# Tying gate units to attention steps, with three smaller moves around them, in a hybrid decoder trunk

## Chip, cores and metric

One Trainium2 chip, one of its cores. The metric is the device time of one launch in microseconds (us), the median of several runs. The engines are called PE (matrix multiplication), DVE (VectorE), ACT (ScalarE), POOL (GpSimd) and SP (SyncE, which here only issues transfers).

## What is computed

One layer of a decoder, for 1024 prompt tokens (NP) and 64 sample tokens (NS) that share the weights. All matrices are float32; the kernel multiplies them as sums of float16 parts, so each matrix product of weights is three matmuls per 128 rows.

```
h = x + 0.5 * g1 * SwiGLU_1(rms(x) * (1 + sc1) + sh1)
u = rms(h) * (1 + sc2) + sh2
[q | k | v | s | ga | gb] = u @ w_in
a = stick-breaking attention(q, k, v)         8 heads x 64, strictly causal
b = GLU(gelu(S5 diagonal SSM(s)))
h = h + g2 * ((sigmoid(ga) * (a @ w_branch_a) + sigmoid(gb) * (b @ w_branch_b)) @ w_out)
h = h + 0.5 * g3 * SwiGLU_2(rms(h) * (1 + sc3) + sh3)
y = final_rms(h)
```

## The kernel before

The program runs as one chain of stages: the first SwiGLU (to about 770 us), the mixer with its projections, SSM, gated linear unit and attention (`mixer_a`, to 1506 us), the mixer's branch products and w_out (`mixer_b`), the second SwiGLU. The order of instructions on each engine is made by a scheduler from the program's order and its dependencies; `tc.issue_after(x)` makes it place what is traced inside behind instruction x. Every engine then runs its own list strictly in that order.

**Weights.** The class `Weights` (L106) holds a list of weight groups. `fetch` loads one by SP into `wf` (two buffers), `measure` takes its largest value (DVE L89, POOL L82, then three small DVE instructions L74 to L76 that make a power-of-two scale), and a split writes `wh` (ACT L101) and `wl` (DVE L102), again two buffers each. `ahead()` brings the next groups to that state.

**Gate units.** The gates ga and gb are 16 units of 128 columns, two to a weight group. `project` (inside `mixer_a`) traces one unit: three chunks of tokens, each 24 matmuls `u<-u,wh` or `u<-u,wl` (L226), 72 in all; ACT evicts each chunk with `gate<-u` (L1339), and a transfer stores it to `gd` in memory (L1340). The 16 units fill holes of other stages: some stand beside the SSM, two before and one inside the gated linear unit (`between`), the remaining eleven go to the attention loop.

**SSM.** `ssm_run` runs in four blocks. Each ends with eight transfers `m<-gp` (L976) that fetch a matrix, matmuls `z<-u,m` (L988, L990), ACT evictions `y<-z` (L992), and eight transfers `yd<-y` (L995) that store the block's result. Both sets of transfers are issued by SP.

**Gated linear unit.** `glu` reads the SSM's result, applies gelu (`zg`), takes its largest value (`zm`), makes the scale `sz` (L74 to L76), splits `zg` into `z` (ACT and DVE L101, L102), and multiplies by two weight groups `glu_w` (PE L226).

**Attention.** `attend_prompt` runs four pairs of heads, two blocks of 512 queries each, and 4 or 8 blocks of keys in each: 48 steps. A step is: logits `z<-qs,kT` (PE L1087, with the causal mask L1092), two evictions by ACT `ae<-z` (L1094) and one each by ACT (L1096) and DVE (L1098), exp and log (ACT L1012, L1013), two DVE instructions (L1014, L1015), a float16 split (ACT L1017, DVE L1021), sums over keys `P<-ah,tri` (PE L1024), `az<-P` (DVE L1026), exp (ACT L1028), sums carried to the next step `P<-ah,earlier` (PE L1103), and the output `o<-az,vt` (PE L1108). Steps overlap: the logits of the next step can run while the last two are still on ACT and DVE. `attend_sample` is traced in pieces between steps.

**The loop around it** pops a gate unit whenever fewer units were popped than the share of steps done times a constant; what is left when the attention ends is traced after it:

```
    while n_gates - len(gates) < (n_gates - 3) * done / steps:
        gates.pop(0)()
```

**Branch products.** `mixer_b` multiplies first branch b (`ob`), then branch a, in units of 36 matmuls (`unit`, L216), with two units in PSUM. Each unit's gate is loaded (`sg<-gd`), ACT applies the sigmoid (L1491), and DVE multiplies product and gate into `mt` (L1495), which frees the unit's PSUM.

Of the kernel before, what the change touches and what calls it, by code (L numbers as in the profile page):

```python
# [9 lines left out]
F32 = mybir.dt.float32  # L10
# [10 lines left out]
P = 128  # L21
# [19 lines left out]
GC = 16  # L41
# [28 lines left out]
def pow2_scale(k, m, pool=None, tag="sc", bufs=8, lead=14):  # L70

    nc = k.nc
    sc = (pool or k.small).tile([P, 2], F32, tag=tag, bufs=bufs)
    nc.vector.tensor_single_scalar(sc[:, 1:2].bitcast(I32), m.bitcast(I32), 0x7F800000, op=ALU.bitwise_and)  # L74
    nc.vector.tensor_scalar(sc[:, 1:2], sc[:, 1:2], 2.0 ** -100, 2.0 ** -lead, op0=ALU.max, op1=ALU.mult)
    nc.vector.reciprocal(sc[:, 0:1], sc[:, 1:2])  # L76
    return sc[:, 0:1], sc[:, 1:2]
# [187 lines left out]
def c3(t):  # L265
    return t.rearrange("p (c n) -> p c n", c=3)
# [642 lines left out]
def ssm_run(k, par, bt, st, ds):  # L909
# [82 lines left out]
            nc.scalar.activation(y.rearrange("p (a g) c -> p g a c", g=2)[:, g2, gas[0]:gas[-1] + 1, :],  # L992
                                 p[:, :len(gas), :], AF.Copy)
    for j in range(TC):
        nc.sync.dma_start(ds["y"][bt, :, j, :].rearrange("(g h) c -> h g c", h=GC), y[GC * j:GC * j + GC])  # L995
    yield


# [70 lines left out]
def attend_prompt(k, qT, kT, vt, pairs, scales):  # L1069

    nc = k.nc
    for p in pairs:
        qs, ks, inv, c = scales[p]
        for qc in range(2):
            acc = k.psa.tile([P, 2, 512], F32, tag="P")
            po = k.pso.tile([P, 512], F32, tag="o")
            top = 4 * qc + 3
            for j in range(top, -1, -1):
                q0 = max(0, P * j - 512 * qc)
                n = 512 - q0  # L1080
                cols = slice(512 * qc + q0, 512 * qc + 512)

                def logits(az, ae):
                    pz = [k.psz.tile([P, 512], F32, tag="z") for _ in range(2)]
                    for i in range(2):
                        for h, ps in enumerate(pz):
                            nc.tensor.matmul(ps[:, :n], ks[:, h, P * j:P * j + P], qs[:, h, i, cols], start=i == 0,  # L1087
                                             stop=True, skip_group_check=True)
                    for h, ps in enumerate(pz):
                        b = k.bias[:, 2 * p + h:2 * p + h + 1]  # L1090
                        if j >= 4 * qc:
                            nc.tensor.matmul(ps[:, :P], k.ident16, k.causal, start=False, stop=True,  # L1092
                                             skip_group_check=True)
                        nc.scalar.activation(ae[:, h, :n], ps[:, :n], AF.Abs, scale=inv, bias=b)  # L1094
                        if h:
                            nc.scalar.activation(az[:, h, :n], ps[:, :n], AF.Identity, scale=inv, bias=b)  # L1096
                        else:
                            nc.vector.tensor_scalar(az[:, h, :n], ps[:, :n], inv, b, op0=ALU.mult, op1=ALU.add)  # L1098

                def rest(hi, lo):  # L1100
                    for h in range(2):
                        for part in (hi, lo):
                            nc.tensor.matmul(acc[:, h, q0:], k.earlier, part[:, h, :], start=False, stop=True,  # L1103
                                             skip_group_check=True)

                w = weights_of(k, n, 2, P, acc[:, :, q0:], logits, rest if j else None, None, j == top, c)
                for h in range(2):
                    nc.tensor.matmul(po[64 * h:64 * h + 64, q0:], vt[:, j, (2 * p + h) * DH:(2 * p + h + 1) * DH],  # L1108
                                     w[:, h, :], start=j == top, stop=j == 0, skip_group_check=True)
                if (qc, j) == (1, 3) and p < 3:  # L1110
                    scales.append(scaled_pair(k, qT, kT, p + 1, (k.qkv, k.ring)[(p + 1) % 2]))
                if j:
                    yield
            o = qT[:, p, 512 * qc:512 * qc + 512]
            nc.scalar.activation(o, po, AF.Copy)
            absmax(k, o, k.mo[:, 2 * p + qc:2 * p + qc + 1])
            yield
# [160 lines left out]
def mixer_a(k, dr, out, u, ivu, par, ds, gd, od):  # L1278
# [6 lines left out]
    def project(g, q, sink, last=False):  # L1285
        if q == 0:
            cur["w"] = k.w.next()
            cur["iv"] = mul_small(k, cur["w"][1], ivu)
        f = sink(2 * g + q, cur["iv"])
        unit_chunks(k, cur["w"], slice(q * P, q * P + P), act, KD, f)  # L1290
        if q and not last:
            k.w.ahead()
# [47 lines left out]
            (nc.gpsimd if m == 15 else nc.sync).dma_start(gd[m, :, c * CH:(c + 1) * CH], t)  # L1340
        return f

    gates = [lambda g=g, q=q: project(g, q, to_gate, g == 7) for g in range(8) for q in range(2)]
    k.gate_slot = lambda: k.ring.tile([P, CH], F32, tag="gs", bufs=2, name="gate")

    def between():
        gates.pop(0)()

    run(2, keep(kT))
    nc.sync.dma_start(out["kT"].rearrange("m p t -> p m t"), kT)  # L1350
# [23 lines left out]
    k.cs_qk = k.co.tile([P, 4, 3], F32, tag="csqk")  # L1374
    k.part_slot = lambda: k.ring.tile([P, NP], F16, tag="r", name="hs")
    scales = [scaled_pair(k, qT, kT, 0, k.qkv)]
    for _ in range(2):
        between()
    ivb = glu(k, dr, ds, od, between)
    k.part_slot = lambda: k.ring.tile([P, 2, 512], F16, tag="h", bufs=4, name="hs").rearrange("p a b -> p (a b)")  # L1380
    first.close()
# [10 lines left out]
    sample = attend_sample(k, dr, qT, kT, vt)  # L1392
    for _ in attend_prompt(k, qT, kT, vt, range(4), scales):
        done += 1
        while n_gates - len(gates) < (n_gates - 3) * done / steps:
            gates.pop(0)()
        if done % 4 == 0:
            next(sample, None)
    for _ in sample:
        pass  # L1400
    for f in gates:
        f()

    n = NP + NS
    s, inv = pow2_scale(k, allmax(k, absmax(k, k.mo)), k.co, "so", 1)
# [7 lines left out]
def glu(k, dr, ds, od, between):  # L1413
# [9 lines left out]
    for m in range(4):  # L1423
# [7 lines left out]
        absmax(k, z, zm[:, 0, m:m + 1])  # L1431
        zg.append(z)
    s, ivz = pow2_scale(k, allmax(k, absmax(k, zm[:, 0, :])), k.co, "sz", 1)
    for m in range(4):
        z2.append(slot([P, 2, T], F16, "z2"))
        split(k, z2[m][:, 0, :], z2[m][:, 1, :], zg[m], s)
# [20 lines left out]
def mixer_b(k, oa, ivo, od, ivb, gd, x, xd, gate, after_chunk):  # L1457
# [25 lines left out]
    for branch, ivx in ((1, ivb), (0, ivo)):  # L1483
        for g in range(2):
            w = k.w.next()
            iv = mul_small(k, w[1], ivx)
            for q in range(4):
                m = 4 * g + q
                sg = k.ring.tile([P, T], F32, tag="r", name="sg")
                nc.sync.dma_start(sg, gd[8 * branch + m])  # L1490
                nc.scalar.activation(sg, sg, AF.Sigmoid)  # L1491
                ps = unit(k, w, slice(q * P, q * P + P), operand[branch], 4)
                if branch:
                    merged.append(slot([P, T], F32, "mt"))
                    v.scalar_tensor_tensor(c3(merged[m]), ps, iv, c3(sg), op0=ALU.mult, op1=ALU.mult)  # L1495
                else:
                    v.scalar_tensor_tensor(c3(sg), ps, iv, c3(sg), op0=ALU.mult, op1=ALU.mult)
                    v.tensor_add(merged[m], merged[m], sg)
                    absmax(k, merged[m], mm[:, m:m + 1])
            if not branch:  # L1500
                half(g)
        if branch:
            for c in range(3):
                nc.sync.dma_start(x[:, :, c * CH:(c + 1) * CH], xd[:, :, c * CH:(c + 1) * CH])
# [323 lines left out]
```

## Time and profile before

| | us |
|---|---|
| median of 3 runs | 2433.33 (2432.96 to 2435.21) |
| profiled execution, its own time | 2430.38 |
| its span | 2428.7 |
| PE busy | 2300.0 (95%) |
| DVE busy | 1663.9 (69%) |
| ACT busy | 966.2 (40%) |
| mean granted clock of PE | 0.977 of full |

Shares of busy time are means over stages. A stage is read from stretches of the span: how long each engine is busy in it, and which wait ends last there. The granted clock is 1.00 at 2.4 GHz and 0.50 at 1.2 GHz; a value between is a stretch with some of each.

### The profile page before, as it was taken

The page shows a single profiled execution, that of the slowest core. Times are in us where ns is not written, and L with a number is a line of the kernel's source. Part 1 is how long each engine was busy: PE and PEld are TensorE (multiplying, and loading weights), DVE is VectorE, ACT ScalarE, POOL GpSimd, SP SyncE. Part 2 cuts the span into 40 slices and gives each one's busy share as a digit, 9 for nine tenths or more (in the row PEclk, how much of TensorE's full clock was granted, in tenths as well). Part 3 has the DMA queues.
Part 4 walks back from the last instruction along what each step waited for, and adds up shares of the span by engine and source line. Part 5 has one row for each costly group of instructions (what it writes and reads, how often), then busy time and mean ns, then how long its engine had stood idle before and what let it go on. Part 6 is the DMA issues. An engine that isn't in the chain of part 4 may idle for free.

```text
span 2428.7 us, 42932 instructions
## 1 busy us (share of the span) xinstructions
PE 2300.0 (95%) x18439; PEld 1631.1 (67%) x18439; DVE 1663.9 (69%) x2994; ACT 966.2 (40%) x1233; POOL 142.3 (6%) x193
## 2 busy tenths in 40 slices
PE   5999999899999999997999977999999999999997
PEld 2677778677787666684545523555688878888884
DVE  4776588877787526435788877597487655677735
ACT  3533331233332422134788877333443321333403
POOL 0000000000000000000332300000000000000000
PEclk8999999999999999998999988999999999999998
DMA  8132334432342154452344413522111133211302
GB/s 306 53 122 101 114 118 140 149 118 109 134 154 105 53 176 112 131 186 102 114 119 131 147 36 110 183 87 86 43 53 53 44 124 109 79 57 53 127 18 75
DMA packets 94191, 262.83 MB, mean 108 GB/s; under 512 B 13152, under 2 KB 50400, under 8 KB 83760
## 3 DMA queue, kind: packets, MB, share of 16 engines
q1 hardware_dynamic: 88240, 242.46, 29.3%
q0 software_dynamic: 5312, 17.34, 2.4%
q8 instruction: 144, 2.36, 0.4%
q14 instruction: 47, 0.39, 0.1%
q10 hardware_dynamic: 448, 0.29, 0.0%
HBM read 204.10 MB, written 49.66 MB: 104 GB/s over the span
## 4 chain that ended last, share of the span: by engine, by line
PE 59%; DVE 11%; ACT 5%; DMA 4%; issue 3%; POOL 1%; SPq 1%; DVEq 0%; POOLq 0%; ACTq 0%
PE u L477 20%; PE u L242 14%; PE u L226 13%; PE u L216 3%; PE z L1364 2%; DVE wl L102 1%; DVE mx L89 1%; DMA wf<-in_w_in 1%; PE P L1024 1%; PE z L990 1%; PE o L1108 1%; PE z L226 1%; ACT ae L1094 1%; PE z L1151 1%; DMA aw<-in_ada_w 1%
## 5 line engine op out<-in xcount | busy, mean ns | idle before, releaser
L226 PE MATMUL u<-u,wh 128*128 128x364 f16 (+1 forms) x1632 | 388.4, 319 | 9.6 <-ACT u L394 6.3
L242 PE MATMUL u<-h,wh 128*128 128x272 f16 (+1 forms) x2304 | 366.8, 281 | 5.2 <-DVE h L102 5.2
L101 ACT ACTIVATE wh<-wf,sc 128x1024 f16<-128x1024 f32 (+2 forms) x128 | 182.4, 1427 | 377.0 <-PE u L242 168.9
L242 PEld LDWEIGHTS <-wh 128*128 128x128 f16 x2816 | 273.8, 97 | 66.1 <-issue 9.0
L89 DVE TENSOR_REDUCE mx<-wf 128x1 f32<-128x1024 f32 (+2 forms) x134 | 211.0, 1597 | 153.0 <-DMA wf<-in_ffn_w_in 78.0
L102 DVE SCALAR_TENSOR_TENSOR wl<-wf,sc,wh 128x1024 f16<-128x1024 f32 (+2 forms) x128 | 208.8, 1631 | 97.7 <-ACT wh L101 97.2
L477 PE MATMUL u<-u,wh 128*128 128x272 f16 x1728 | 273.2, 280 | 0.3 <-DVE q L499 0.3
L477 PEld LDWEIGHTS <-wh 128*128 128x128 f16 x2304 | 221.5, 97 | 64.1 <-issue 20.3
L226 PEld LDWEIGHTS <-wh 128*128 128x128 f16 x1824 | 176.9, 98 | 130.4 <-issue 28.9
L226 PE MATMUL u<-u,wl 128*128 128x364 f16 (+1 forms) x816 | 259.9, 319 | 1.1 <-DVE wl L102 1.1
L242 PE MATMUL u<-h,wl 128*128 128x274 f16 (+1 forms) x1152 | 228.8, 280 | 0.0
L477 PEld LDWEIGHTS <-w3h 128*128 128x128 f16 x1728 | 167.1, 97 | 39.0 <-issue 4.5
L477 PE MATMUL u<-fac,w3h 128*128 128x272 f16 (+1 forms) x1152 | 182.7, 280 | 0.0
L477 PE MATMUL u<-u,wl 128*128 128x272 f16 x864 | 170.5, 279 | 0.0
L82 POOL PARTITION_ALL_REDUCE am<-mx x106 | 55.7, 532 | 1924.8 <-DVE mx L89 1845.5
L242 PEld LDWEIGHTS <-wl 128*128 128x128 f16 x1408 | 136.8, 97 | 29.6
L226 PEld LDWEIGHTS <-wl 128*128 128x128 f16 x912 | 89.3, 98 | 61.0 <-issue 6.9
L477 PEld LDWEIGHTS <-wl 128*128 128x128 f16 x1152 | 111.6, 97 | 24.5 <-issue 0.4
L226 PEld LDWEIGHTS <-aside 128*128 128x128 f16 x864 | 83.0, 97 | 50.5 <-issue 1.7
L477 PE MATMUL u<-fac,w3l 128*128 128x272 f16 x576 | 114.0, 279 | 0.0
L503 ACT ACTIVATE h<-h,iv 128x546 f32<-128x546 f32 x36 | 27.0, 749 | 205.8 <-DVE h L502 205.8
L477 PE MATMUL u<-fac,wh 128*128 128x272 f16 x576 | 92.3, 283 | 4.7 <-DVE st L519 4.7
(429 smaller groups left out, 3893.1 us busy)
## 6 DMA issues: line engine op xcount, KB each, us to landing
wf<-in_ffn_w_in SPq DMA_DIRECT2D x44, 1024.0 KB, 4.7
aw<-in_ada_w SPq DMA_DIRECT2D x72, 512.0 KB, 4.6
wf<-in_w_in SPq DMA_DIRECT2D x16, 1024.0 KB, 5.0
wf<-in_ffn_w_out_a SPq DMA_DIRECT2D x16, 640.0 KB, 4.0
xd<-xr SPq DMA_DIRECT2D x16, 546.0 KB, 2.7
x<-xd SPq DMA_DIRECT2D x16, 546.0 KB, 7.3
xd<-x SPq DMA_DIRECT2D x6, 1456.0 KB, 7.4
sg<-gd SPq DMA_DIRECT2D x16, 546.0 KB, 3.6
```

Of the source, the lines that this page charges most:

```text
L82: k.nc.gpsimd.partition_all_reduce(r, m, P, ABSMAX)
L89: k.nc.vector.tensor_reduce(m, src, axis=axis, op=ALU.max, apply_absolute_value=True)
L101: r = k.nc.scalar.activation(hi, src, AF.Copy, scale=s)
L102: k.nc.vector.scalar_tensor_tensor(lo, src, s, hi, op0=ALU.mult, op1=ALU.subtract)
L216: k.nc.tensor.matmul(ps[:, c, :n], wt[:, cols], act(kt, part)[:, c * CH:c * CH + n], start=kt == 0 and j == 0, stop=kt == nk - 1 and j == 2)
L226: k.nc.tensor.matmul(ps[:, :n], wt[:, cols], act(kt, part)[:, c * CH:c * CH + n], start=kt == 0 and j == 0, stop=kt == nk - 1 and j == 2)
L242: k.nc.tensor.matmul(ps[:, a:b], wt[:, cols], act(kt, part)[:, a0 + a:a0 + b], start=kt == 0 and j == 0, stop=kt == nk - 1 and j == 2)
L477: nc.tensor.matmul(t[:, c0:c1], wt[:, kt * P:kt * P + P], act(kt, part)[:, c0 - 240:c1 - 240], start=first and kt == 0 and j == 0, stop=kt ...
L503: nc.scalar.activation(h2, h2, AF.Silu, scale=iv)
L990: nc.tensor.matmul(p[:, q, :], ca[rows, ri, ga, 1:, :].rearrange("p a b -> p (a b)"), x[rows, ga, :], start=False, stop=ri == 1)
L1024: nc.tensor.matmul(acc[:rk, h, :], k.tri[:rk, :rk], part[:, h, :], start=first and j == 0, stop=True, skip_group_check=True)
L1364: nc.tensor.matmul(ps[:M, :256], u[:, kt, part, tt * P:tt * P + M], wt, start=kt == 0 and j == 0, stop=kt == KD - 1 and j == 2)
```

## The change

Four edits. (1) The SSM's stores `yd<-y` are issued by ACT instead of SP. (2) `attend_prompt` remembers the last logits matmul it traced (`k.anchor`), and a gate unit popped in the attention loop is placed behind it; the loop's constant changes so that nine units are popped inside and two after it, and these two are tied to the last logits as well. (3) The second unit before the gated linear unit no longer requests weights; `glu` does that itself once it has made `sz`. (4) In branch b, the first two units are evicted by ACT into `mt` with the scale, and the gate is multiplied in later; a tile `gap` takes 128 columns of the ring.

```diff
--- before.py
+++ after.py
@@ -992,7 +992,7 @@
             nc.scalar.activation(y.rearrange("p (a g) c -> p g a c", g=2)[:, g2, gas[0]:gas[-1] + 1, :],
                                  p[:, :len(gas), :], AF.Copy)
     for j in range(TC):
-        nc.sync.dma_start(ds["y"][bt, :, j, :].rearrange("(g h) c -> h g c", h=GC), y[GC * j:GC * j + GC])
+        nc.scalar.dma_start(ds["y"][bt, :, j, :].rearrange("(g h) c -> h g c", h=GC), y[GC * j:GC * j + GC])
     yield
 
 
@@ -1084,8 +1084,8 @@
                     pz = [k.psz.tile([P, 512], F32, tag="z") for _ in range(2)]
                     for i in range(2):
                         for h, ps in enumerate(pz):
-                            nc.tensor.matmul(ps[:, :n], ks[:, h, P * j:P * j + P], qs[:, h, i, cols], start=i == 0,
-                                             stop=True, skip_group_check=True)
+                            k.anchor = nc.tensor.matmul(ps[:, :n], ks[:, h, P * j:P * j + P], qs[:, h, i, cols],
+                                                        start=i == 0, stop=True, skip_group_check=True).ins
                     for h, ps in enumerate(pz):
                         b = k.bias[:, 2 * p + h:2 * p + h + 1]
                         if j >= 4 * qc:
@@ -1340,11 +1340,11 @@
             (nc.gpsimd if m == 15 else nc.sync).dma_start(gd[m, :, c * CH:(c + 1) * CH], t)
         return f
 
-    gates = [lambda g=g, q=q: project(g, q, to_gate, g == 7) for g in range(8) for q in range(2)]
+    gates = [lambda g=g, q=q, last=False: project(g, q, to_gate, last or g == 7) for g in range(8) for q in range(2)]
     k.gate_slot = lambda: k.ring.tile([P, CH], F32, tag="gs", bufs=2, name="gate")
 
-    def between():
-        gates.pop(0)()
+    def between(**kw):
+        gates.pop(0)(**kw)
 
     run(2, keep(kT))
     nc.sync.dma_start(out["kT"].rearrange("m p t -> p m t"), kT)
@@ -1374,8 +1374,8 @@
     k.cs_qk = k.co.tile([P, 4, 3], F32, tag="csqk")
     k.part_slot = lambda: k.ring.tile([P, NP], F16, tag="r", name="hs")
     scales = [scaled_pair(k, qT, kT, 0, k.qkv)]
-    for _ in range(2):
-        between()
+    between()
+    between(last=True)
     ivb = glu(k, dr, ds, od, between)
     k.part_slot = lambda: k.ring.tile([P, 2, 512], F16, tag="h", bufs=4, name="hs").rearrange("p a b -> p (a b)")
     first.close()
@@ -1392,14 +1392,16 @@
     sample = attend_sample(k, dr, qT, kT, vt)
     for _ in attend_prompt(k, qT, kT, vt, range(4), scales):
         done += 1
-        while n_gates - len(gates) < (n_gates - 3) * done / steps:
-            gates.pop(0)()
+        while n_gates - len(gates) < (n_gates - 2) * done / steps:
+            with tc.issue_after(k.anchor):
+                gates.pop(0)()
         if done % 4 == 0:
             next(sample, None)
     for _ in sample:
         pass
     for f in gates:
-        f()
+        with tc.issue_after(k.anchor):
+            f()
 
     n = NP + NS
     s, inv = pow2_scale(k, allmax(k, absmax(k, k.mo)), k.co, "so", 1)
@@ -1431,6 +1433,7 @@
         absmax(k, z, zm[:, 0, m:m + 1])
         zg.append(z)
     s, ivz = pow2_scale(k, allmax(k, absmax(k, zm[:, 0, :])), k.co, "sz", 1)
+    k.w.ahead()
     for m in range(4):
         z2.append(slot([P, 2, T], F16, "z2"))
         split(k, z2[m][:, 0, :], z2[m][:, 1, :], zg[m], s)
@@ -1488,10 +1491,18 @@
                 m = 4 * g + q
                 sg = k.ring.tile([P, T], F32, tag="r", name="sg")
                 nc.sync.dma_start(sg, gd[8 * branch + m])
-                nc.scalar.activation(sg, sg, AF.Sigmoid)
                 ps = unit(k, w, slice(q * P, q * P + P), operand[branch], 4)
                 if branch:
+                    if m == 0:
+                        k.ring.tile([P, 128], F32, tag="gap", bufs=1)
                     merged.append(slot([P, T], F32, "mt"))
+                early = branch and m < 2
+                if early:
+                    nc.scalar.activation(c3(merged[m]), ps, AF.Copy, scale=iv)
+                nc.scalar.activation(sg, sg, AF.Sigmoid)
+                if early:
+                    v.tensor_mul(merged[m], merged[m], sg)
+                elif branch:
                     v.scalar_tensor_tensor(c3(merged[m]), ps, iv, c3(sg), op0=ALU.mult, op1=ALU.mult)
                 else:
                     v.scalar_tensor_tensor(c3(sg), ps, iv, c3(sg), op0=ALU.mult, op1=ALU.mult)
```

How the lists of the engines move is shown at three places.

ACT, fourth pair of heads, second block of queries, from the exp of the 384-wide step on; `ae<-z` is the eviction of a step's logits, `gate<-u` that of a gate chunk. Before:

```order
L1012 ACTIVATE ae<-ae 128x2x384
L1094 ACTIVATE ae<-z,bias,csqk 128x512
L1013 ACTIVATE ae<-ae 128x2x384
L1094 ACTIVATE ae<-z,bias,csqk 128x512
L1028 ACTIVATE az<-az 128x2x256
L1096 ACTIVATE az<-z,bias,csqk 128x512
L1017 ACTIVATE ah<-ae,csqk 128x2x384
L1012 ACTIVATE ae<-ae 128x1024
```

And now:

```order
L1012 ACTIVATE ae<-ae 128x2x384
L1013 ACTIVATE ae<-ae 128x2x384
L1339 ACTIVATE gate<-u,iv 128x364
L1028 ACTIVATE az<-az 128x2x256
L1017 ACTIVATE ah<-ae,csqk 128x2x384
L1028 ACTIVATE az<-az 128x2x384
L1339 ACTIVATE gate<-u,iv 128x364
L101 ACTIVATE wh<-wf,sc 128x2048
L1339 ACTIVATE gate<-u,iv 128x364
L1094 ACTIVATE ae<-z,bias,csqk 128x512 x2
```

The steps in flight now run to their last exp (`az<-az`), and the three chunks of a gate unit are evicted, before the next step's logits. On PE the 72 gate matmuls of such a unit stand in the same place: behind one step's logits, between the `P` and `o` matmuls of the steps in flight, and all before the logits of the next. There are eight such units; the last gate matmuls in a row directly before the next logits are 36, 2, 49, 3, 25, 18, 31 and 24. Before, gate matmuls stood spread among logits, `P` and `o` from the start of the attention, and the last of them well before its end. Of the last two units 53 matmuls now stand among the last steps and 91 in a row between the last `o` and the first branch product (L216); before, the branch product followed the last `o` directly.

DVE, at the gated linear unit; `wl<-wf` is a weight's low part, `mx<-wf` the measure of one, `sz` the scale. Before, after the last `zm<-zg`:

```order
L89 TENSOR_REDUCE mx<-zm 128x1
L102 SCALAR_TENSOR_TENSOR wl<-wf,sc,wh 128x1024
L89 TENSOR_REDUCE mx_11754<-wf 128x1
L74 TENSOR_SCALAR sc<-am 128x1
L75 TENSOR_SCALAR sc<-sc 128x1
L76 RECIPROCAL sc<-sc 128x1
L102 SCALAR_TENSOR_TENSOR wl<-wf,sc,wh 128x1024
L89 TENSOR_REDUCE mx_11938<-wf 128x1
L74 TENSOR_SCALAR sc<-am 128x1
L74 TENSOR_SCALAR sz<-am 128x1
```

And now:

```order
L102 SCALAR_TENSOR_TENSOR wl<-wf,sc,wh 128x1024
L89 TENSOR_REDUCE mx_11754<-wf 128x1
L74 TENSOR_SCALAR sc<-am 128x1
L74 TENSOR_SCALAR sz<-am 128x1
```

The second `wl` and the second measure no longer stand ahead of `sz`; one measure still does. On PE the gate units, the gated linear unit and the unit inside it now follow each other as 360 matmuls of L226 in a row.

SP, around the last two SSM blocks. Before, from the third block's `m<-gp` on:

```order
L976 DMA m_10547<-gp 16x8x128 x8
L978 DMA ca<-ca 128x1152
L926 DMA m_10558<-m_88 128x1024
L928 DMA ph<-ph 128x1024
L995 DMA yd<-y 16x8x136 x8
L122 DMA wf<-in_w_in 128x2048
L995 DMA yd<-y 16x8x136 x8
L976 DMA m_10984<-gp 16x8x128 x8
```

And now:

```order
L976 DMA m_10547<-gp 16x8x128 x8
L978 DMA ca<-ca 128x1152
L926 DMA m_10558<-m_88 128x1024
L928 DMA ph<-ph 128x1024
L1340 DMA gd<-gate 128x364 x2
L122 DMA wf<-in_glu_w 128x1024
L1372 DMA out_fins<-fins 128x256
L1371 DMA out_fin<-fin 128x32
L976 DMA m_10984<-gp 16x8x128 x8
```

The last block's `m<-gp` stood behind sixteen stores and a weight; now it stands behind two gate stores, another weight and the stores of the final states. On PE 24 more gate matmuls stand ahead of that block's products.

## Rows read from the trace of the kernel before

**Rows 1.** Page, part 1: busy time, share of the span, instructions

```profile
PE 2300.0 (95%) x18439; PEld 1631.1 (67%) x18439; DVE 1663.9 (69%) x2994; ACT 966.2 (40%) x1233; POOL 142.3 (6%) x193
```

**Rows 2.** Stretches: length; busy PE, PEld, DVE, ACT, POOL; clock; DMA share; GB/s

```profile
1153.00:1420.00 267.00, 257.12 (x1857) 133.82 (x1858) 221.74 (x299) 224.82 (x335) 80.56 (x73) 0.99 0.41 123
1420.00:1506.40 86.40, 57.77 (x275) 21.66 (x268) 66.41 (x75) 65.00 (x91) 1.09 (x2) 0.81 0.21 79
...
1433.00:1506.40 73.40, 47.90 (x191) 17.21 (x192) 54.77 (x62) 55.86 (x77) 0.00 (x0) 0.80 0.23 86
```

**Rows 3.** Waits of PE, 860 to 1506 us: total, times, longest

```profile
PE u L226 <- ACT z L101: 11.9, 1, 11.9
...
PE z L988 <- DMA m<-gp: 4.7, 1, 4.7
```

**Rows 4.** Timeline of DVE, 1062 to 1108 us: start, length, instruction, wait before

```profile
1073.79 0.16 DVE L89 TENSOR_REDUCE mx<-zm 128x1 f32<-128x4 f32 x1
...
1083.63 2.29 DVE L89 TENSOR_REDUCE mx<-wf 128x1 f32<-128x2048 f32 x1 [8.48 <-DMA wf<-in_w_in]
```

**Rows 5.** Stretches at half clock, behind the gated linear unit's wait and two others

```profile
1106.40:1110.40 4.00, 3.68 (x12) 1.66 (x12) 4.00 (x4) 3.98 (x4) 0.00 (x0) 0.50 0.00 0
1014.80:1022.60 7.80, 7.52 (x27) 4.92 (x28) 0.00 (x0) 1.66 (x3) 0.00 (x0) 0.50 0.54 187
1523.20:1527.60 4.40, 4.40 (x15) 2.17 (x15) 1.16 (x1) 1.52 (x2) 0.00 (x0) 0.50 1.06 397
```

**Rows 6.** Timeline of SP's transfers, 1003 to 1016 us

```profile
1005.17 3.62 SPq L995 DMA_DIRECT2D yd<-y  x8
1008.88 3.70 SPq L976 DMA_DIRECT2D m<-gp  x8
```

**Rows 7.** Timeline of PE: gate matmuls (four apart), and parts of one attention step

```profile
1093.25 0.32 PE L226 MATMUL u<-u,wh 128*128 128x360 f16 x1
...
1093.86 0.32 PE L226 MATMUL u<-u,wl 128*128 128x360 f16 x1
...
1448.23 0.38 PE L1024 MATMUL P<-ah,tri 128*128 128x512 f16 x1
1448.45 0.39 PE L1024 MATMUL P<-ae,tri 128*128 128x512 f16 x1
1451.30 1.12 PE L1108 MATMUL o<-az,vt 128*64 128x512 f32 x2 [2.46 <-ACT az L1028]
```

**Rows 8.** Timeline of ACT, 1500 to 1532 us: the branch products' first sigmoids

```profile
1520.59 4.12 ACT L1491 ACTIVATE sg<-sg 128x1092 f32<-128x1092 f32 x4
```

**Rows 9.** Waits of PE, 1500 to 1532 us

```profile
PE u L216 <- DVE mt L1495: 5.0, 1, 5.0
```

**Rows 10.** Waits of ACT, 1433 to 1506 us

```profile
ACT az L1028 <- DVE az L1026: 8.2, 4, 3.8
ACT qT L1115 <- PE o L1108: 4.1, 2, 2.1
ACT ae L1094 <- PE z L1092: 2.1, 2, 1.9
```

**Rows 11.** Groups of ACT instructions, 1153 to 1506 us: count, busy, mean, idle before

```profile
L1094 ACT ACTIVATE ae<-z,bias,csqk 128x512 f32<-128x512 f32 (+3 forms) x96 | 62.8, 669 | 17.4 <-PE z L1092 10.3 <-PE z L1087 4.4 <-DMA od<-ob 2.6
...
L1017 ACT ACTIVATE ah<-ae,csqk 128x1024 f16<-128x1024 f32 (+3 forms) x48 | 45.0, 938 | 6.9 <-DVE ae L1014 6.5
...
L1013 ACT ACTIVATE ae<-ae 128x1024 f32<-128x1024 f32 (+4 forms) x53 | 43.7, 825 | 0.3
L1012 ACT ACTIVATE ae<-ae 128x1024 f32<-128x1024 f32 (+4 forms) x53 | 43.6, 822 | 0.1
...
L1028 ACT ACTIVATE az<-az 128x1024 f32<-128x1024 f32 (+3 forms) x48 | 40.5, 845 | 12.9 <-DVE az L1026 12.6
...
L1096 ACT ACTIVATE az<-z,bias,csqk 128x512 f32<-128x512 f32 (+3 forms) x48 | 32.2, 671 | 0.0
...
L1339 ACT ACTIVATE gate<-u,iv 128x364 f32<-128x364 f32 x33 | 18.2, 571 | 5.1 <-PE u L226 5.1
```

## The prediction

> **What bounds the kernel now.** I read the page's busy shares first. PE works 95% of the span [rows 1], so a saving must either be a hole on PE or make PE's work pass faster; the change adds and removes almost no matmuls. Then the stretches [rows 2], to find where that share is lower, and PE's waits [rows 3], to see what ends the holes. From 1153 to 1420 us, where gate units fill the attention, PE is busy 257.12 of 267 us at clock 0.99. From 1420 to 1506.4, after the last gate unit, it is busy 57.77 of 86.4 at clock 0.81. Outside the attention two long waits of the mixer stand out: 11.9 us before the gated linear unit and 4.7 us in the SSM [rows 3]; a third, 5.0 us, comes after the attention [rows 9]. The change touches all four places. The attention is by far the largest and the least certain.
>
> **Gated linear unit: -13.9 us.** What PE waits for is `z`, thus `sz`. Its input was ready on DVE at 1073.79, but the second weight's `wl` and a measure stand ahead of `sz`. Now only the measure that ran at 1083.63 is ahead of it, and it ended 2.29 us later, about 1086 [rows 4]. The split of `z` then takes place while PE still has gate matmuls, and PE goes on without a hole. The 11.9 us go. PE also ran at half clock for 4.0 us afterwards [rows 5], which cost half of that, 2.0: together -13.9. The second weight's split is late next; 72 matmuls with the first weight cover it. A gate matmul takes 0.152 us (four of them from 1093.25 to 1093.86 [rows 7]), so that is 10.9 us against an ACT and a DVE instruction. If the cover is not enough, up to 3 us come back.
>
> **SSM: -1 us, between -8 and +3.** The last block's `m<-gp` was issued right behind eight stores that took SP 3.62 us and itself took 3.70 [rows 6]; PE waited 4.7 us and then ran 7.8 us at half clock, 3.9 lost [rows 3, 5]. All of both would be 8.6; I cap the gain at 8. But the transfer now stands behind a weight and the final states' stores, which themselves wait, and ACT spends the 3.6 us for eight stores ahead of its evictions: +3 as the other end. Part of the hole should go, because 24 matmuls (3.6 us) now stand ahead of it; I take -1, near a balance of the two, since a new wait replaces the old. The Trainium skill, "DMA: Bandwidth & Descriptors", section "Issuing engines are not separate DMA queues", says that transfers from several engines share the same 16 DMA engines and only the issuing time is saved. By that rule the move alone would give at most the 3.62 us of issue here and nothing of transfer time, so the sum would lie nearer zero gain than -8; no row of this trace shows these stores on ACT.
>
> **End of the attention: +6.6 us, between +3 and +10.** 91 gate matmuls stand alone after the last `o`: 91 x 0.152 = 13.8 us, where the branch product followed at once. Part of it can hide the chain from `o` to the next scale, but that chain was hidden behind branch b already, so nothing is saved there. In exchange the third branch unit waits only for ACT's copy, no longer for four sigmoids (4.12 us [rows 8]) and DVE: the 5.0 us wait [rows 9] and the half clock after it (4.4 us, 2.2 lost [rows 5]) go, 7.2 in all. 13.8 - 7.2 = 6.6.
>
> **Attention: +1.1 us, between -16 and +28.** With 72 gate matmuls placed whole between one step's logits and the next's, PE is no longer what counts: ACT is, and its holes. ACT is busy 224.82 + 65.00 = 289.8 us of 353.4 [rows 2]. Six of its gate evictions at 0.571 [rows 11] move behind the attention: 286.4 remain. Holes without gate units are read from the gate-free stretch: 17.5 of 73.4 us [rows 2], of which 8.2 + 4.1 + 2.1 = 14.4 [rows 10] lie where a block of queries ends. I count that once, and the other 3.1 in 59 us, 5%, over all the work: 14.5. That gives 286.4 + 14.4 + 14.5 = 315.3, plus 8 units times x, the time that ACT stands empty at each.
>
> For x: from logits to logits PE needs 72 x 0.152 = 10.9 us and the `P` and `o` matmuls of the steps in flight. Eight `P` at 0.22 and four `o`, two of them 1.12 overlapped and at half clock, so about 0.25 each, make 2.8 us a step [rows 7]: 13.7 us with one step, 16.5 with two. ACT has, when the logits end, one step's work of (62.8 + 32.2 + 43.6 + 43.7 + 45.0 + 40.5) / 48 = 5.6 us, and 0.94 + 0.85 + 0.85 of the two before it [rows 11]: 8.2, up to 10.9 with three gate evictions (1.7) and half a weight's split (1.0). So x lies between 13.7 - 10.9 = 2.8 and 16.5 - 8.2 = 8.3. I take 4.9, somewhat nearer the low end, because in four of eight units 25 or fewer matmuls are left in a row before the next logits, so that ACT has been fed until shortly before. 315.3 + 8 x 4.9 = 354.5, against 353.4: +1.1; the ends give 337.7 (-15.7) and 381.7 (+28.3). So the idle PE time at the end of the attention is used, and nearly all of it is paid again as idle ACT time at the units.
>
> **Sum.** -13.9 - 1 + 6.6 + 1.1 = -7.2 us on the profiled execution's own 2430.38, thus 2423.2; that execution lay 2.95 below the median of the runs, 2433.33, so I forecast 2433.3 - 7.2 = **2426.1, rounded to 2426 us**. A measurement of this kernel can tell about 0.2%, 4.9 us, from no change.
>
> **Rivals.**
> (a) *The steps run dry* (slower, 0.22). The next logits are queued behind 72 gate matmuls, ACT and DVE empty, and the two steps must be refilled. With x at 7.3, well toward its upper end, the attention takes 315.3 + 58.4 = 373.7, 19.2 more than forecast, the whole +12.0: 2445 us. It decides the sign from x = 4.9 + 7.2 / 8 = 5.8 on. For it: before, the trace shows `P`, `o` and ACT waiting on each other with gates absent [rows 10]. Against it: the long hole of PE in the step shown is 2.46 us [rows 7], much less than x here.
> (b) *The units start at half clock* (slower, 0.08). After each wait in rows 5 PE ran 4.0 to 7.8 us at 1.2 GHz, having been idle 4.7 to 11.9 us. If each of the eight units starts so after a thin stretch, 8 x 2.0 = 16 us come on top: 2442. Against it: the waits inside the attention are shorter, and the clock is 0.99 while gates are there [rows 2]. The Trainium skill, "TensorE: Matmul & The Clock Gate", section "HAM oscillation", describes this pattern: bursts of matmuls divided by waits, each burst beginning cold. By that rule all eight would pay; the trace agrees only for the gate-free stretch, at clock 0.80.
> (c) *`sz` stays late* (slower, 0.05). One measure still stands ahead of it, and it had waited 8.48 us for a weight [rows 4]. If that weight is now requested about 10 us later, the wait stays: 2426.1 + 13.9 = 2440.
> (d) *The gates hide* (faster, 0.20). With x at 2.8, PE and ACT both stay fed: attention -15.7, 16.8 less than forecast, total -24.0, 2409 us. For it: ACT has 63.6 us of holes in the attention to be used [rows 2].
>
> **How the numbers follow.** The forecast case, x between about 4 and 5.8, has 0.45, of which 0.25 lies below the 0.2% bound and 0.20 within it. Faster is 0.25 + 0.20 = 0.45, same 0.20, slower 0.22 + 0.08 + 0.05 = 0.35. The forecast's own range is 2419 to 2433. The range for eight in ten reaches from (d) with the SSM's best end, 2409 - 7 = 2402, to 2450, which leaves out the upper part of (a): its end, x at 8.3, would be 2433.3 - 7.2 + 27.2 = 2453.
>
> **What would show it.** Right: PE's wait for `z` before the gated linear unit is gone and its clock stays 1.00 there; no 5 us wait for `mt`; about 13.8 us of L226 between the last `o` and L216; the attention, from the first `ae<-z` to the last `o`, within 5 us of 353; ACT's waits for logits grow from 17.4 us [rows 11] to over 40; the clock of the last 86 us rises above 0.9. Wrong: an attention over 365 or under 345 us (x is mis-sized), a clock below 0.9 during gate units (b), a wait for `z` of over 5 us (c), or a PE wait for `m<-gp` longer than 4.7 us.

## The result, and the profile after

The change makes the kernel slower: 2516.52 us (2513.51 to 2519.64) against 2433.73, a ratio of 1.034 with an interval of 1.0322 to 1.0357. The forecast was 2426 us, with a range of 2402 to 2450. It is outside the range, on the other side.

The page's first part after the change, as [rows 1] before:

```profile
PE 2341.3 (93%) x18439; PEld 1647.6 (66%) x18439; DVE 1664.6 (66%) x2994; ACT 974.4 (39%) x1235; POOL 141.1 (6%) x193
```

PE has the same number of instructions and is busy 41 us longer; its mean granted clock fell from 0.977 to 0.958, so more of the same work ran at half clock. The span grew by 86.6 us, from 2428.7 to 2515.3. The stretch of the attention, from the first `ae<-z` to the last `o`, with the columns of [rows 2]:

```profile
1149.00:1583.10 434.10, 340.13 (x2052) 160.87 (x2051) 289.74 (x374) 292.05 (x420) 79.24 (x72) 0.83 0.26 77
```

Before, the same stretch was 352.9 us long (1153.0 to 1505.9). ACT and DVE do the same work as in [rows 2] (292.05 against 289.8, 289.74 against 288.15). What grew is the time in which they stand empty: on ACT from 63 to 142 us. The clock fell from 0.94 to 0.83.

By stages, the 86.6 us are:

| | us |
|---|---|
| before the attention (it starts at 1149.0 instead of 1153.0) | -4.0 |
| the attention, 434.0 against 352.9 | +81.1 |
| from the last `o` to the first branch product, 14.0 against 0.5 | +13.5 |
| from there to the end, 918.3 against 922.3 | -4.0 |

Inside the attention the loss is concentrated. The lines of DVE's timeline with `az<-P` (one per step, L1026) around the first and the last of eight gaps:

```profile
1197.34 0.75 DVE L1026 SCALAR_TENSOR_TENSOR az<-P,csqk,az 128x512 f32<-128x512 f32 x1 [0.59 <-PE P L1024]
1216.60 1.02 DVE L1026 SCALAR_TENSOR_TENSOR az<-P,csqk,az 128x768 f32<-128x768 f32 x1 [3.39 <-PE P L1024]
...
1535.37 1.02 DVE L1026 SCALAR_TENSOR_TENSOR az<-P,csqk,az 128x768 f32<-128x768 f32 x1 [0.75 <-PE P L1024]
1556.43 1.28 DVE L1026 SCALAR_TENSOR_TENSOR az<-P,csqk,az 128x1024 f32<-128x1024 f32 x1
```

There are eight such gaps, one at each of the eight units, of 16.3 to 21.1 us; together they are 150 us. A step took 353 / 48 = 7.4 us before, so eight ordinary gaps would have taken 59. The difference, 91 us, is a little more than the whole loss of the attention. The mean hides a spread, though: before, single gaps were up to 19.5 us long, and the eight longest were 106 us together.

One of the gaps as a stretch of all engines, from one step's logits at 1335.30 to the next ones at 1354.06:

```profile
1335.30:1354.10 18.80, 18.79 (x106) 9.48 (x105) 17.25 (x21) 12.85 (x15) 4.92 (x4) 1.00 0.61 161
```

PE is busy 18.79 of 18.80 us, at full clock. By busy share and clock this stretch is perfect. Yet behind the logits with which it opens it contains none, and that is what the attention waits for. The eight stretches from the end of one step's logits on PE to the start of the next are 13.9 to 18.0 us long, 15.9 in the mean, about what I had worked out (13.7 to 16.5), and their clock is 0.88 to 1.00. The first, the last and the sum of all eight:

```profile
1189.85:1204.94 15.09, 15.09 (x96) 8.87 (x95) 5.88 (x20) 5.78 (x12) 0.00 (x0) 0.91 0.07 25
...
1524.76:1541.82 17.06, 17.06 (x109) 9.73 (x107) 7.86 (x10) 8.10 (x13) 0.00 (x0) 0.93 0.07 23
sum 127.16, PE 126.75 PEld 70.34 DVE 72.85 ACT 67.62 POOL 5.38; mean PE 15.84 PEld 8.79 DVE 9.11 ACT 8.45 POOL 0.67
```

PE has holes of 0.4 us in all of them together; ACT stands empty for 127.16 - 67.62 = 59.5 us, 7.4 at each unit. How it goes on behind the last unit shows in ACT's timeline (the next logits began on PE at 1541.82):

```profile
1541.87 2.00 ACT L101 ACTIVATE wh<-wf,sc 128x2048 f16<-128x2048 f32 x1 [3.85 <-PE u L226]
1543.78 0.55 ACT L1339 ACTIVATE gate<-u,iv 128x364 f32<-128x364 f32 x1
1544.22 1.44 ACT L1094 ACTIVATE ae<-z,bias,csqk 128x512 f32<-128x512 f32 x2
```

ACT was empty for 3.85 us, then did a weight split and a gate eviction, and only at 1544.22 the logits. The next `az<-P` is at 1556.43, 14.6 us after the logits. That stretch:

```profile
1541.82:1556.43 14.61, 6.40 (x21) 2.13 (x19) 11.15 (x10) 14.29 (x17) 1.40 (x1) 0.70 0.24 85
```

Now ACT is full, with the split, the gate eviction and the evictions of three steps' logits, and PE is the engine that waits, at clock 0.70. In the first 10 us behind each of the eight units, 80 us in all, ACT is busy 72.5 us and PE 48.2:

```profile
sum 80.00, PE 48.17 PEld 21.26 DVE 48.69 ACT 72.48 POOL 8.66; mean PE 6.02 PEld 2.66 DVE 6.09 ACT 9.06 POOL 1.08
```

ACT's waits in the attention, summed by what ended them (compare [rows 10], which cover a part of it):

```profile
ACT az L1028 <- DVE az L1026: 34.7, 23, 4.3
ACT gate L1339 <- PE u L226: 29.2, 18, 3.1
ACT ah L1017 <- DVE ae L1014: 17.5, 13, 8.1
ACT wh L101 <- PE u L226: 14.3, 4, 3.9
```

Before the attention, PE's waits from 860 to 1149 us, against [rows 3]:

```profile
PE z L988 <- ACT vt L1366: 5.0, 1, 5.0
PE z L990 <- DMA ca<-ca: 2.2, 1, 2.2
```

The 11.9 us for `z` are gone, as forecast. The wait in the SSM is still there. The view puts it down to ACT, whose `vt<-z` ended at 1025.25; but the last of the eight `m<-gp` landed at 1025.25 too. On SP they now stand behind the stores of the final states, which waited 7.2 us (`out_fins`) and 3.7 us (`out_fin`) for DVE:

```profile
1018.64 0.34 SPq L1371 DMA_DIRECT2D out_fin<-fin  x1
1019.03 4.14 SPq L976 DMA_DIRECT2D m<-gp  x8
```

And the branch products, against [rows 9]:

```profile
PE u L216 <- ACT mt L1501: 1.4, 1, 1.4
PE u L216 <- DMA ob<-od: 0.6, 1, 0.6
```

### The profile page after: what moved, and what is told of

It is laid out like the page before. It is cut to its first block, busy times and chain, and to the rows that moved or that the text cites. A ratio compares the mean times of both kernels' runs of the same rounds, so it can differ in the third digit from the quotient of the medians.

```text
span 2515.3 us, 42938 instructions
## 1 busy us (share of the span) xinstructions
PE 2341.3 (93%) x18439; PEld 1647.6 (66%) x18439; DVE 1664.6 (66%) x2994; ACT 974.4 (39%) x1235; POOL 141.1 (6%) x193
## 4 chain that ended last, share of the span: by engine, by line
PE 39%; DVE 6%; ACT 5%; issue 1%; DMA 1%; POOL 1%; DVEq 0%; SPq 0%; POOLq 0%; ACTq 0%
PE u L477 13%; PE u L242 9%; PE u L226 8%; PE u L216 3%; PE o L1108 1%; PE P L1024 1%; ACT ae L1094 1%; PE z L1087 1%; PE P L1103 1%; PE z L1151 1%; DVE az L1026 1%; DMA xd<-x 1%; DVE ae L1014 1%; ACT ae L1013 0%; DVE mx L89 0%
## 5 line engine op out<-in xcount | busy, mean ns | idle before, releaser
L226 PE MATMUL u<-u,wh 128*128 128x364 f16 (+1 forms) x1632 | 388.5, 321 | 9.5 <-ACT u L394 6.3
L242 PEld LDWEIGHTS <-wh 128*128 128x128 f16 x2816 | 273.2, 97 | 67.0 <-issue 10.2
L226 PE MATMUL u<-u,wl 128*128 128x364 f16 (+1 forms) x816 | 262.0, 321 | 1.1 <-DVE wl L102 1.1
L226 PEld LDWEIGHTS <-wh 128*128 128x128 f16 x1824 | 177.9, 98 | 119.0 <-issue 17.3
L226 PEld LDWEIGHTS <-wl 128*128 128x128 f16 x912 | 89.7, 98 | 62.5 <-issue 8.7
L226 PEld LDWEIGHTS <-aside 128*128 128x128 f16 x864 | 82.9, 97 | 51.3 <-issue 1.7
```

What stands on the lines that cost most here:

```text
L226: k.nc.tensor.matmul(ps[:, :n], wt[:, cols], act(kt, part)[:, c * CH:c * CH + n], start=kt == 0 and j == 0, stop=kt == nk - 1 and j == 2)
L242: k.nc.tensor.matmul(ps[:, a:b], wt[:, cols], act(kt, part)[:, a0 + a:a0 + b], start=kt == 0 and j == 0, stop=kt == nk - 1 and j == 2)
```

## Experiments

Each ratio is to the kernel before on the same chip, whose median moved between 2429.7 and 2437.8 from one set to the next. "Attention" is the length from the first `ae<-z` to the last `o` in the profiled execution.

### Which edit costs what

**The change without the tie.** Edit 2 taken back, the others kept:

```diff
-        while n_gates - len(gates) < (n_gates - 2) * done / steps:
-            with tc.issue_after(k.anchor):
-                gates.pop(0)()
+        while n_gates - len(gates) < (n_gates - 3) * done / steps:
+            gates.pop(0)()
```

> The change without its second edit: gate units are popped and placed as before, the other three edits stay. Theory (the tie is the loss: the next logits stand behind 72 gate matmuls, which costs about 81 us in the attention and 14 us after it): the time falls from 2516 to about 2429, near before; inside that the stores on ScalarE cost about 13 us in the SSM, the later weight request saves about 14, the early eviction about 4. Rival (the attention is slow for another reason, such as the weights requested later arriving late for the gate units): the time stays near 2500.

Measured: 2424.16 us, ratio 0.9936 (0.9924 to 0.9949), attention 358.5. The whole loss is in the tie, and the other three edits together gain 0.6%.

**The tie alone**, the converse:

> The kernel before with the second edit alone (gate units behind a step's last logits, nine in the loop, two after). Theory: nearly all of the loss is here, 2433 + 81 + 14 = about 2528. Rival (the loss needs the other edits, for instance late weights): under 2450.

Measured: 2546.4 us, ratio 1.0443 (1.0425 to 1.0461), attention 454.7. The theory holds and the rival falls; the loss is even larger than forecast, 12.7 us for each of the eight units in the attention. That edit 2 costs less inside the change (434.0) goes for the most part with waits in this trace that the change's doesn't have: 17.6 us of ACT for which the view names no releaser on this core ("remote").

```profile
ACT rows L1195 <- remote: 11.1, 3, 5.9
ACT ae L1094 <- remote: 6.5, 2, 5.9
```

Counted out they leave 437 us, 10.5 for each unit. What they wait for is open. The traces of the change without the tie, of the stores on ScalarE alone and of edits 3 and 4 have 7.8 us of such waits each, the others none; these four were measured in the set in which the kernel before was slowest (2437.8).

**The stores on ScalarE alone:**

```diff
-        nc.sync.dma_start(ds["y"][bt, :, j, :]...
+        nc.scalar.dma_start(ds["y"][bt, :, j, :]...
```

> The kernel before with the SSM's stores issued by ScalarE and nothing else. Theory (ScalarE spends 4 to 8 us at each set of eight stores and the evictions behind them wait, so PE stalls in the SSM): slower by 8 to 13 us, 2441 to 2446. Rival (the SSM lost its 13 us because the list of SyncE was reordered by the other edits, not because of ScalarE): within 5 us of 2433.

Measured: 2444.28 us against 2437.77, ratio 1.0025 (1.0016 to 1.0035), thus 6.1 us slower, between the two. Its ACT timeline shows the cost:

```profile
1011.41 8.65 ACTq L995 DMA_DIRECT2D yd<-y  x8
1020.11 0.56 ACT L1339 ACTIVATE gate<-u,iv 128x364 f32<-128x364 f32 x1 [8.27 <-DMA yd<-y]
1020.57 0.83 ACT L1366 ACTIVATE vt<-z,iv 128x256 f32<-128x256 f32 x2
```

The eight stores hold ACT's list for 8.65 us, where SP needed 3.62 [rows 6], and ACT stands empty for 8.27 us until the eviction behind them starts. In the change the view lets an eviction `vt<-z` that stands behind these stores end PE's 5.0 us wait above. But what ends PE's wait in this experiment is the transfer, and in the change without the tie as well; first the one, then the other:

```profile
PE z L988 <- DMA m<-gp: 5.3, 1, 5.3
```

```profile
PE z L988 <- DMA m<-gp: 6.1, 1, 6.1
```

On SP `m<-gp` stands behind the final states' stores in both, as in the change. So moving the stores to ScalarE had two effects, evictions that start later and a fetch that is issued later, and these runs don't separate them.

**Edits 3 and 4**, together and each alone:

> The kernel before with edits 3 and 4 alone (later weight request in the gated linear unit, first two branch products evicted early). Theory: the 11.9 us wait for z and the half clock behind it go (14 us), and the 5.0 us wait for mt goes with 4 to 7 us: 2433 - 18 to 21 = 2412 to 2415. Rival (the savings are given back in the attention, which starts earlier but whose gate units are then fed later): 2425 or more.

> The kernel before with edit 3 alone, the later weight request. Theory: the wait of 11.9 us and the half clock behind it go, -12 to -14 us (2419 to 2421). Rival (most of what edits 3 and 4 gave came from edit 4): over 2426.

> The kernel before with edit 4 alone, the two early evictions. Theory: the part behind the attention shrinks by 4 to 6 us as it did in the change, 2427 to 2429. Rival: no change, since the sigmoids and loads that the eviction no longer waits for stop the next unit instead, 2431 to 2435.

Measured: together 2420.29 us, ratio 0.9919 (0.9906 to 0.9932), 20 us; edit 3 alone 0.9946 (0.9934 to 0.9958), 13 us; edit 4 alone 0.9981 (0.9972 to 0.9989), 4.6 us. The theories hold in all three. Edit 4 leaves, in place of the 5.0 us [rows 9], this wait of PE:

```profile
PE u L216 <- ACT mt L1498: 0.8, 1, 0.8
```

### Why the tie costs so much

The next four tie gate work in the same way on top of edits 3 and 4, with the stores on SP, but in pieces of different size. Their foot is edits 3 and 4 untied, whose attention is this stretch:

```profile
1141.90:1501.90 360.00, 318.44 (x2126) 156.31 (x2124) 288.33 (x374) 290.06 (x425) 82.53 (x75) 0.94 0.35 110
```

> The change with the stores back on SyncE: edits 2, 3 and 4 (units of 72 gate matmuls tied to steps). It is the foot of the next two, which tie smaller pieces. Both theories: the tie alone cost 113 us, edits 3 and 4 save 17 to 20: 2433 + 113 - 18 = about 2528.

> The same, but the loop ties pieces of two chunks (48 gate matmuls, 7.3 us at full clock) to steps, so that fifteen pieces stand between logits instead of eight; 7 matmuls are left behind the last o. Theory A (each piece drains the steps in flight, whatever its size, at some 11 us): 2420 + 15 x 11 = about 2585, slower than units. Theory B (what counts is how much longer the piece is than the work ScalarE and VectorE still have, about 8 us): 2425 to 2460.

> The same with single chunks (24 gate matmuls, 3.6 us): thirty pieces between logits, 24 matmuls behind the last o. Theory A: 2420 + 30 x 11 = about 2750. Theory B: 3.6 us fit into the work pending, so the attention loses nothing at a piece and gains the gate-free stretch at its end: 2405 to 2430, about the same as edits 3 and 4 without a tie (2420).

> Edits 3 and 4, with the loop's gate work tied in pieces of half a chunk: 12 gate matmuls, 1.8 us, one or two of them at every step; 6 matmuls behind the last o. The cost of a piece in the attention, against edits 3 and 4 untied (360 us), was 9.4 us with 72 matmuls, 4.1 with 48, 1.2 with 24. Theory B (the cost is the piece's excess over the work pending): it goes to about zero with 12 and the spread of the gate work over the whole attention is left, 2405 to 2425. Rival (a tie as such keeps about 1 us a piece, since the gate work is kept from the holes it would have filled): 2440 to 2470.

The pieces are made so (for single chunks; for half chunks `product` is called for four of the eight `kt` at a time, and the loop's constant is 3 for single and 4 for half chunks):

```diff
+            for c in range(3):
+                def piece(g=g, q=q, c=c):
...
+                    unit_chunk(k, cur["w"], slice(q * P, q * P + P), act, KD, c, to_gate(2 * g + q, cur["iv"]))
```

| piece | us | ratio | attention | above untied, per piece | per 72 matmuls |
|---|---|---|---|---|---|
| 72 matmuls, 8 before the last logits | 2508.0 | 1.0317 (1.0294 to 1.034) | 435.6 | 9.5 | 9.5 |
| 48, 15 | 2489.62 | 1.0231 (1.0208 to 1.0254) | 425.6 | 4.4 | 6.6 |
| 24, 30 | 2464.31 | 1.013 (1.0108 to 1.0152) | 399.1 | 1.3 | 3.9 |
| 12, 62 | 2442.83 | 1.0045 (1.0032 to 1.0058) | 383.9 | 0.4 | 2.3 |

Their stretches of the attention; first 72, then 48, 24 and 12 matmuls:

```profile
1140.90:1576.50 435.60, 337.10 (x2036) 158.43 (x2034) 288.88 (x372) 291.96 (x420) 79.92 (x72) 0.84 0.25 75
```

```profile
1141.70:1567.30 425.60, 339.44 (x2136) 165.78 (x2136) 289.64 (x372) 293.34 (x423) 74.68 (x74) 0.88 0.29 87
```

```profile
1141.30:1540.40 399.10, 326.94 (x2143) 161.52 (x2142) 289.18 (x372) 294.34 (x423) 74.53 (x74) 0.92 0.30 92
```

```profile
1141.60:1525.50 383.90, 329.14 (x2161) 163.69 (x2160) 288.37 (x372) 291.28 (x423) 75.70 (x74) 0.91 0.32 96
```

The untied trace contains one wait of 6.1 us that the tied ones don't have, of the kind named above:

```profile
1380.90 0.69 ACT L1195 ACTIVATE rows<-z,bias_r 128x512 f32<-128x512 f32 x1 [6.11 <-remote]
```

With it counted out (353.9) the costs per piece are 10.2, 4.8, 1.5 and 0.5; the order stays. With whole units 576 gate matmuls stand between logits, with the smaller pieces 720 to 744, so the rows differ in that too.

DVE and ACT are busy the same time in all of them, within 1.5%; only the length changes. Theory A (each piece drains the steps at a fixed price) falls: the cost of a piece drops from 9.5 to 0.4. Theory B has the direction right, but not the point at which the cost ends: pieces of 3.6 us, well under the work pending, still cost 1.3 us each, and its times for 48 and 24 matmuls (up to 2460 and 2430) were missed by 30 and 34 us. Even the finest tie loses 24 us to no tie at all. So the rival of the last experiment has the direction (its 2440 to 2470 was met, its price of about 1 us a piece was not): a tie as such costs a little, at every size tried. What exactly it costs there is not settled.

**The matmuls or the unit.** For the last two kernels the gate products of the loop keep only the first of their three matmuls. This leaves out the low parts of the products.

```diff
-        for j, (wt, part) in enumerate(passes(w, kt)):
+        for j, (wt, part) in enumerate(passes(w, kt)[:1 if k.short else 3]):
```

> The kernel before, with the gate units of the attention loop cut to the first of their three matmuls (24 per unit instead of 72; evictions, stores and weights stay). It leaves out the low parts of those gate products. Untied, it is the foot of the next one: 480 matmuls x 0.152 = 73 us of PE work less, of which the attention gives back what was not hidden: 2380 to 2425.

> The same cut (the low parts of the loop's gate products are left out) with edit 2: whole units, now of 24 matmuls, tied to steps, with their three evictions and the weight split in the same places of ScalarE's list. If the cost of 9 us a unit is PE's time for 72 matmuls, it falls to 1 or 2 us a unit: 8 to 16 us above the untied one. If it comes with the unit as such (steps in flight drained, evictions and a weight split ahead of the next logits), it stays at 6 us or more a unit: 50 us or more above.

The untied one took 2435.84 us, ratio 1.0029 (1.0018 to 1.0041); the tied one 2473.79, 1.0174 (1.0157 to 1.0191). Their attention, untied and then tied:

```profile
1156.80:1509.20 352.40, 261.52 (x1639) 114.32 (x1638) 287.13 (x375) 288.73 (x424) 78.32 (x75) 0.86 0.36 113
```

```profile
1156.10:1541.50 385.40, 274.89 (x1639) 119.67 (x1638) 286.42 (x374) 289.17 (x424) 75.88 (x75) 0.82 0.30 89
```

The untied one was expected at 2380 to 2425 and missed it. Two things follow. First, the untied line: with 480 matmuls less the attention takes 352.40 us, where the kernel before took 352.9. So two thirds of PE's gate work in the holes were free as far as this cut can tell. It is not a clean reading: the clock is lower than before (0.86 against 0.94), and ACT has a wait for the gate stores that the kernel before doesn't have:

```profile
ACT gate L1340 <- DMA gd<-gate: 11.7, 5, 3.4
```

Second, the tie costs 33.0 us here, 4.1 for each of the eight units, against 12.7 with whole units on the same foot, or 10.5 without the waits of no named releaser. So about three fifths to two thirds of the price go with PE's time for the 48 matmuls left out, and 4.1 us stay with the unit as it then is, its last 24 matmuls included. The measurement lies between the two expected cases. The tied kernel lost 11.6 us more behind the attention, where nothing covered a late load:

```profile
PE u L217 <- DMA ob<-od: 11.6, 1, 11.6
```

### A version that beats both

**The stores on GpSimd**, with edits 3 and 4 and no tie:

```diff
-        nc.sync.dma_start(ds["y"][bt, :, j, :]...
+        nc.gpsimd.dma_start(ds["y"][bt, :, j, :]...
```

> Edits 3 and 4, with the SSM's stores issued by GpSimd in place of ScalarE or SyncE. Theory (ScalarE's issue time was what cost 6 to 13 us in the SSM): GpSimd has nothing else there, so the loss is gone and the 4.7 us wait shrinks: 2412 to 2420. Rival (the list of SyncE, reordered as soon as the stores leave it, puts the last block's fetch behind gate stores and a weight): still 4 to 10 us slower than edits 3 and 4, 2424 to 2430.

Measured: 2401.6 us (2400.74 to 2403.91) against 2430.47, ratio 0.9877 (0.9862 to 0.9891), better than expected. GpSimd issues the stores in about 4.2 us a set:

```profile
1015.38 4.17 POOL L995 DMA_DIRECT2D yd<-y  x8 [5.75 <-ACT y L992]
```

and PE's waits from 860 to 1140 us hold no `m<-gp` any more; these are all of them:

```profile
PE u L226 <- ACT qT L1311: 1.8, 1, 1.8
PE z L942 <- ACT y L992: 1.7, 1, 1.7
PE u L226 <- DVE wl L102: 1.1, 1, 1.1
```

SP's list is reordered here too, with the last `m<-gp` behind gate stores and a weight, so that part of the reordering is not what cost in the change. But here the fetch stands ahead of the final states' stores, and it is issued 8.4 us earlier than in the change (1019.03 there):

```profile
1010.61 4.84 SPq L976 DMA_DIRECT2D m<-gp  x8
```

So two things differ from the change, the engine that issues the stores and the place of the fetch on SP, and which of them gains the time is not shown. Besides the SSM its attention is shorter than with edits 3 and 4 alone (352.2 against 360.0); 6.1 us of that is the wait for no named releaser, which this trace doesn't have.

## Why the prediction was wrong

**Attention, forecast +1.1, measured +81.1.** This is the step that failed. That PE's place between the logits would make ACT stand empty was right; the sum of ACT's work and its empty time was not. By its terms, the measured ones from the stretches of the result:

| | forecast | measured | miss |
|---|---|---|---|
| ACT's work | 286.4 | 292.05 | +5.7 |
| ACT empty outside the units | 14.4 + 14.5 = 28.9 | 142.0 - 59.5 = 82.5 | +53.6 |
| ACT empty at the eight units, 8 times x | 39.2 | 59.5 | +20.3 |
| the attention | 354.5 | 434.1 | +79.6 |

The larger error is the second row. The holes of 14.4 us at the end of a block of queries were counted once, though the attention has eight blocks, and the rest as 5% of the work. Yet the prediction itself names 63.6 us of holes on ACT in the attention before (in rival (d)), and with two thirds of the gate matmuls cut away ACT is still empty for 352.4 - 288.7 = 63.7 us [the untied line above]. So 34.7 of the 53.6 us were there before the change and were left out. I took the stretch from 1433 to 1506 us [rows 2] as a sign that PE's idle time there could be won; ACT and DVE waited there as well, in the chain of a step. The other 18.9 us came with the tie, outside the units. That the steps run at a lower clock behind a unit, with PE waiting, fits; how much each part costs no experiment separates.

The third row is x: forecast 4.9, bounds 2.8 and 8.3, measured 7.4 in the mean and 4.8 to 9.8 at single units. PE's time between logits was about right. What was too large is the work that I let ACT do meanwhile, 8.2 to 10.9 us, as if all that was pending could run. Part of it waits for `P` matmuls that now stand between gate matmuls in PE's list, which fits `az`'s wait for DVE's `az<-P`, grown from 12.6 us in all to 34.7. ACT's waits for gate matmuls (`gate` and `wh`) grew from 5.1 to 43.5. The prediction's reason for a low x was also misread from its own list: five of the eight units, not four, have 25 matmuls or fewer in a row, and x came out high all the same.

Two of its signs failed with it. ACT's waits for logits are 20.3 us, not over 40, and the last 86 us of the attention stay at clock 0.80, not above 0.9:

```profile
L1094 ACT ACTIVATE ae<-z,bias,csqk 128x512 f32<-128x512 f32 (+3 forms) x96 | 62.5, 664 | 20.3 <-PE z L1092 12.5 <-PE z L1087 7.2 <-PE P L1103 0.2
```

```profile
1497.00:1583.10 86.10, 65.32 (x307) 29.14 (x305) 55.99 (x61) 58.27 (x78) 1.40 (x1) 0.80 0.07 24
```

Rival (a) had the mechanism, place and sign, and its x of 7.3 is close to the measured 7.4; it was given 0.22 and 2445 us, because it stood on the same 315.3. Rival (b), half clock at the start of the units, has the wrong place: at the eight units the clock is 0.88 to 1.00, which by their lengths is an estimated 5 us, not 16. The clock falls behind them and takes the attention's mean to 0.83. Rival (d) falls.

**Gated linear unit, forecast -13.9.** Right: no wait for `z`, and edit 3 alone gave 13 us (10 to 16). One measure ahead of `sz` did no harm, so rival (c) falls.

**SSM, forecast -1, bounds -8 and +3.** Wrong in sign and just outside the bounds: 6.1 us (3.9 to 8.5) with that edit alone; the change reached the attention 4.0 us earlier, so of the 13 us from edit 3 about 9 were lost here; the last block's first product came at 1025.39 instead of 1014.85. I bounded ACT's share by SP's issue time, 3.6 us for eight stores. On ACT a set took 4.2 to 8.7 us, with the evictions behind it. The other end of my +3, the fetch behind the final states' stores on SP, was undersized too: it was issued at 1019.03 instead of 1008.88 and landed in the same moment in which ACT's eviction ended. With the stores on GpSimd both are avoided, so which of the two cost the time stays open. The Trainium skill's "DMA: Bandwidth & Descriptors", section "Issuing engines are not separate DMA queues", says that issuing elsewhere saves only issue time, usually small beside the transfer. Here that time was not small on ScalarE: eight stores held its list for 8.65 us and the eviction behind them waited 8.27.

**End, forecast +6.6.** The 91 matmuls, 90 of which have a record, cost what was worked out:

```profile
1583.12 13.93 PE u L226 x90
```

The early evictions gave back 4.0 us in the change and 4.6 alone, instead of 7.2: with 13.5 from `o` to branch product, +9.5. Within its bounds; a wait of 1.4 us for ACT's copy and 0.6 for a load stayed.

## What to carry to other kernels

Filler work that a scheduler spreads through another stage's holes can be nearly free even when its engine looks full; before moving it, take it out and time the stage without it, which shows whether there is anything to win. A block of filler placed in front of the instruction that starts the next step makes the other engines stand empty, and PE can be 100% busy at full clock meanwhile. When a stage's time is summed from one engine's work and holes, hold the sum against the holes that the trace has in all (here 63.6 us against 28.9). When transfers are moved to another queue, look at what stands behind them on the engine that will issue them, and at what the queue they leave then issues first.

## What was not expected

With two thirds of the loop's gate matmuls left out (73 us of PE's time), the kernel was not faster but slightly slower, 1.0029: the attention stayed at 352.40 us while its clock fell from 0.94 to 0.86, and it began 3.8 us later than in the trace before, though nothing ahead of it was changed. A set of eight stores took SP 3.6 to 4.3, GpSimd 4.2 to 4.5 and ScalarE 4.2 to 8.65 us to issue.
